# Output product of two channel mixers: gated values stationary, weights moving, 14 of 22 inner tiles in seven block products

## The chip, the cores and the metric

The kernel runs on one core of one Trainium2 chip. Its time is device time of one execution in microseconds (us). The engines are TensorE (PE: matmuls and their weight loads, PEld), VectorE (DVE), ScalarE (ACT), GpSimd (POOL) and SyncE (SP), which here issues most transfers. All matrix products are float32 work done as three products of parts: each operand is split into a high part (type fp32r) and the rest, and high x high, high x low and low x high are summed in PSUM.

## The reference

A trunk of two layers for 512 tokens of width 1024. Layer 0 mixes tokens by a recurrent scan beside a memory attention; layer 1 by chunked attention beside a memory attention. Each layer ends with the channel mixer, which is what the change is about:

```python
def conv_glu(h, w_in, conv_w, conv_b, w_out):
    gate, val = jnp.split(h @ w_in, 2, axis=-1)
    gp = jnp.pad(gate, ((0, 0), (CONV_W - 1, 0), (0, 0)))
    conv = conv_b + sum(conv_w[j] * gp[:, j:j + seq] for j in range(CONV_W))
    return (jax.nn.gelu(conv, approximate=False) * val) @ w_out
...
        x = x + jnp.concatenate([mix, mo], axis=-1) @ w_out[layer]
        x = x + conv_glu(rms_norm(x, ln2[layer]), ffn_in[layer], ffn_conv[layer],
                         ffn_conv_b[layer], ffn_out[layer])
    return rms_norm(x, ln_f)
```

The inner width is 2816 = 22 tiles of 128, so the last product of the mixer is a [512 x 2816] by [2816 x 1024] product.

## The kernel before

Everything is kept with features on partitions: the residual `xT` is [128, 8, 512], eight tiles of 128 features by 512 tokens. `ffn(l, ...)` is a generator that serves both layers. Its first half takes 21 of the 22 inner tiles through class `Seven`: for each tile seven block products of 128x256 stand for the gate and value products (lines 412 and 414), and a frame of hand-placed steps (`keep` pins their order on each queue) prepares the next tile's weights, while the gate chains of the tiles before (`end1` to `end5`: rho, three convolution taps, Gelu, times value) run on VectorE and ScalarE. The gated tiles are stored in float32: tiles 0 to 6 in `sp`, 7 to 13 in `x32[1]`, 14 to 21 in `x32[0]`. `rho`, the reciprocal root mean square of each token, is left out of the value branch and applied to the result.

`ending()` carries the last frame, the 22nd tile by plain products (`pg`, `pv`), the splits of all 22 gated tiles into high and low parts (`highs` on ScalarE, line 601; `lows` on VectorE, line 605), and the first weight units of the output product. Then the output product runs over the eight output tiles `m`: three units of weights with 7, 8 and 7 inner tiles are loaded (`raw_w`, line 192), split (line 173 on ScalarE, line 181 on VectorE, two units with an accumulating transfer at line 179), and `dense` multiplies them: weights stationary, gated values moving, 512 tokens wide, 66 matmuls for one `m` (lines 219, 220, 223). The result is multiplied by `rho` (line 731), added to `xT` (732), and `after(m)` squares and sums it for the next norm and, in layer 0, splits it for the queries of layer 1 (lines 270 to 278).

In layer 0 the attention layer begins behind that: two query projections of 24 matmuls each (`pq`), the norm's sums over features by matmuls with a column of ones (line 289), its transposes (302), the shared key and value operand (`kv_operand`), the key projection. In layer 1 `finish` takes the eighth tile in two halves of 256 tokens: the first half's norm and output run beside the second half's products (`store`), and the second half is turned by transposes (1731) and stored with tokens on partitions. So the two halves of the output have different layouts, which the host puts together.

[...] Split weights live in three buffers each of `whi` and `wlo`, 1024 columns long, raw weights in two of `wraw`. Outside the pinned stretches the framework orders each queue by priority (the order of the listing) among what its model holds ready.

Of the kernel before, what the change touches and what calls it, by code (L numbers as in the profile page):

```python
# [18 lines left out]
P = 128  # L19
S = 512  # L20
# [95 lines left out]
def trunk_kernel(ctx, tc, A, out):  # L116
# [278 lines left out]
    def ffn(l, hp, U, T, new_x, xT, after, last=None):  # L395
# [177 lines left out]
        hid = {}  # L573

        outs = {}
        UNITS = ((8, 7), (0, 8), (15, 7))

        def out_unit(m, u, pin=None):
            o, n = UNITS[u]
            src = A["ffn_out"][l, m][:, o * P:(o + n) * P]  # L580
            raw = raw_w(src, n * P)
            if m:
                return split_w(raw, n * P, None, pin or (lambda i: i)), list(range(o, o + n))
            return split_w(raw, n * P, src if u < 2 else None, keep, hold=True), list(range(o, o + n))

        def ending():
# [6 lines left out]
            hl = [hp.tile([P, 7, S], F32R, name="hl", tag="raw", bufs=2) for _ in range(2)]  # L593

            def place(k):
                return [t[:, k - 8] for t in hl] if k > 7 else (Th[:, k], Tl[:, k])

            def highs(*ks):
                for k in ks:
                    hid[k] = place(k) if k < 15 else (xh[:, k - 15], sl[:, k - 15])  # L600
                    keep(SC.copy(hid[k][0], hid32[k]))

            def lows(*ks):
                for k in ks:
                    keep(V.tensor_tensor(hid[k][1], hid32[k], hid[k][0], op=ALU.subtract))

            highs(8, 9)
# [3 lines left out]
            lows(8, 9)  # L611
# [4 lines left out]
            highs(10, 11, 12)  # L616
            lows(10)
            yield
            highs(13)
            yield  # L620
            pg = ps_f()
# [5 lines left out]
            lows(11)  # L627
            highs(0)
# [3 lines left out]
            highs(1, 14)  # L632
# [3 lines left out]
            lows(12)  # L636
            pv = ps_f()
# [7 lines left out]
            highs(7)  # L645
            u0 = out_unit(0, 0)
            u0[0][2]()
            lows(13, 14, 7)
            tile21.end3()
            tile21.end3b()  # L650
            highs(2, 3)
            lows(0, 1, 2)
            u1 = out_unit(0, 1)
            tile21.end4()
            highs(4, 5, 6)
            u1[0][2]()
            lows(3, 4, 5, 6)
            xh = new_x(1, F32R)
            sl = hp.tile([P, 7, S], F32R, name="sl", tag="sp")
            highs(15, 16, 17)  # L660
            tile21.end5()
            lows(15, 16, 17)
            u2 = out_unit(0, 2)
            highs(*range(18, NFF))
            lows(*range(18, NFF))
            u2[0][2]()
            outs[0] = [(w[:2], ks) for w, ks in (u0, u1, u2)]
            outs[1] = [out_unit(1, u, keep if u == 0 else None) for u in range(3)]
            yield

# [52 lines left out]
        for m in range(KD):  # L723
            us = outs[m] if m < len(outs) else [out_unit(m, u) for u in range(3)]
            if m == KD - 1 and last is not None:
                last(us, lambda k: hid[k])
                break
            ps = ps_d()
            run(dense(ps[:], us, lambda k: hid[k]))
            o = tmp()  # L730
            V.tensor_tensor(o[:], ps[:], rho[:], op=ALU.mult)
            V.tensor_tensor(xT[:, m], xT[:, m], o[:], op=ALU.add)
            after(m)
# [711 lines left out]
    def new_t():  # L1445
        return [hp.tile([P, KD, S], F32R, name="t" + u, tag="t" + u) for u in "hl"]

    mixer = ffn(0, hp, (r2h, r2l), new_t(), lambda i, dt: new_r(i, 1, dt), xT,
                lambda m: norm_tile(xT[:, m], m, "ln1_1", r2h, r2l))
    with fctx:  # L1450
        next(mixer)
# [391 lines left out]
```

## Time and profile before

| | |
|---|---|
| median of 3 runs | 1319.76 us (1319.14 to 1319.88) |
| profiled execution, its own time | 1320.44 us |
| its span | 1318.7 us |
| granted TensorE clock | 0.998 |
| PE busy | 1295.3 us (98%) |
| DVE busy | 980.1 us (74%) |
| ACT busy | 789.0 us (60%) |
| moved by DMA | 170.51 MB, mean 129 GB/s |

The span runs from the first to the last instruction of the profiled execution; its own time has some 1.7 us around that. A row of a timeline gives the start, the time, engine, line, operation, output and inputs, and in brackets the idle time before it with what ended it. A row of groups gives the count, the busy time and the mean of one in ns, then the idle time before. A duration of a matmul reaches to its modelled end; matmuls overlap, so the pace is read from starts.

### The profile page before, as it was taken

Reading aid. Unit: us, or ns where it says so; the run is one execution under the profiler, and the core shown is the slowest. Engines: PE = TensorE matmul, PEld = TensorE weight load, DVE = VectorE, ACT = ScalarE, POOL = GpSimd, SP = SyncE. Lnnn points to the kernel's source line nnn. Section 1 sums busy time; section 2 is a strip of 40 time slices with the busy share of each in tenths; the row PEclk is TensorE's granted clock in tenths of the full one; section 3 lists DMA queues with packets and bytes.
Section 4 is the critical chain, followed back from the end, with each engine's and each line's share of the span. In section 5 each row is a group of like instructions: output and inputs, shape, how many; then the busy total and the mean of one; then the engine's idle time right before and its main releaser. Section 6 shows DMA issues by size and latency. Waiting matters only on the chain.

```text
span 1318.7 us, 26462 instructions
## 1 busy us (share of the span) xinstructions
PE 1295.3 (98%) x10578; PEld 1122.7 (85%) x10578; DVE 980.1 (74%) x1933; ACT 789.0 (60%) x1318; POOL 113.2 (9%) x133
## 2 busy tenths in 40 slices
PE   9999999999999999999999999999999999999998
PEld 7887777767789999998888888787799999997887
DVE  7966867665689999999444666748889999995334
ACT  6656656655566776768223467757657767674321
POOL 0000000000001221220000000000012212200000
PEclk9999999999999999999999999999999999999999
DMA  6375344351236788776333432232447887855332
GB/s 200 109 191 112 88 90 104 87 114 58 95 97 160 178 198 183 173 174 150 106 99 107 136 98 79 86 107 88 128 105 178 197 180 175 198 126 139 101 99 78
DMA packets 87659, 170.51 MB, mean 129 GB/s; under 512 B 21232, under 2 KB 29552, under 8 KB 87536
## 3 DMA queue, kind: packets, MB, share of 16 engines
q1 hardware_dynamic: 67296, 124.94, 30.6%
q0 software_dynamic: 20240, 43.88, 19.8%
q8 instruction: 83, 1.36, 0.4%
q14 instruction: 40, 0.33, 0.1%
HBM read 152.57 MB, written 6.29 MB: 120 GB/s over the span
## 4 chain that ended last, share of the span: by engine, by line
PE 81%; ACT 7%; DVE 7%; DMA 2%; issue 2%; SPq 0%; DVEq 0%; ACTq 0%
PE psf L412 21%; PE psd L223 11%; PE psd L219 11%; PE psd L220 10%; PE psf L414 10%; PE pss L1593 1%; DVE wlo L181 1%; PE pss L1252 1%; PE psf L220 1%; PE psf L219 1%; PE pss L929 1%; ACT whi L173 1%; PE pss L1263 1%; PE pss L348 1%; PE psf L223 1%
## 5 line engine op out<-in xcount | busy, mean ns | idle before, releaser
L173 ACT CAST whi<-wraw 128x1024 fp32r<-128x1024 f32 (+1 forms) x116 | 118.0, 1020 | 198.5 <-DMA wraw<-in_ffn_out_dram 135.4
L181 DVE TENSOR_TENSOR wlo<-wraw,whi 128x1024 fp32r<-128x1024 f32 (+1 forms) x93 | 109.6, 1179 | 127.3 <-PE psd L223 72.4
L466 ACT CAST whi<-raw 128x1024 fp32r<-128x1024 f32 (+1 forms) x168 | 153.6, 941 | 71.7 <-PE psf L412 37.0
L412 PE MATMUL psf<-tl,whi 128*128 128x256 f32 x672 | 168.7, 283 | 0.0
L412 PE MATMUL psf<-th,whi 128*128 128x256 f32 x672 | 168.4, 283 | 0.0
L471 DVE TENSOR_TENSOR wlo<-raw,whi 128x1024 fp32r<-128x1024 f32 (+1 forms) x126 | 131.5, 1044 | 14.6 <-ACT whi L466 14.1
L412 PEld LDWEIGHTS psf<-tl,whi 128*128 128x128 f32 x672 | 128.9, 192 | 0.0
L412 PEld LDWEIGHTS psf<-th,whi 128*128 128x128 f32 x672 | 128.7, 192 | 0.0
L219 PE MATMUL psd<-r1h,whi 128*128 128x512 f32 x248 | 101.5, 410 | 0.1
L220 PE MATMUL psd<-r1l,whi 128*128 128x512 f32 x248 | 97.9, 396 | 0.0
L414 PE MATMUL psf<-th,wlo 128*128 128x256 f32 x504 | 81.2, 283 | 0.0
L223 PE MATMUL psd<-r1h,wlo 128*128 128x512 f32 x248 | 72.3, 407 | 0.0
L414 PEld LDWEIGHTS psf<-th,wlo 128*128 128x128 f32 x504 | 69.7, 192 | 0.0
L449 POOL DMA_DIRECT2D wlv<-in_ffn_in_dram x40 | 61.3, 1533 | 59.1 <-DVE tmp L533 58.3
L412 PE MATMUL psf<-r2h,whi 128*128 128x256 f32 x252 | 63.3, 283 | 0.5 <-ACT whi L466 0.5
L412 PE MATMUL psf<-r1h,whi 128*128 128x256 f32 x252 | 63.3, 283 | 0.5 <-ACT whi L466 0.5
L412 PE MATMUL psf<-r2l,whi 128*128 128x256 f32 x252 | 63.2, 283 | 0.0
L412 PE MATMUL psf<-r1l,whi 128*128 128x256 f32 x252 | 63.2, 283 | 0.0
L219 PEld LDWEIGHTS psd<-r1h,whi 128*128 128x128 f32 x248 | 46.5, 188 | 12.0 <-issue 2.8
L492 ACT ACTIVATE tmp<-tmp,vec 128x512 f32<-128x512 f32 x44 | 35.9, 816 | 34.1 <-DVE tmp L479 32.8
L220 PEld LDWEIGHTS psd<-r1l,whi 128*128 128x128 f32 x248 | 46.6, 188 | 8.1 <-issue 0.2
L223 PEld LDWEIGHTS psd<-r1h,wlo 128*128 128x128 f32 x248 | 44.1, 188 | 9.7 <-issue 1.2
(525 smaller groups left out, 3477.1 us busy)
## 6 DMA issues: line engine op xcount, KB each, us to landing
raw<-in_ffn_in_dram SPq DMA_DIRECT2D x42, 512.0 KB, 3.8
raw<-in_ffn_in_dram SPq DMA_DIRECT2D x84, 256.0 KB, 4.2
wlv<-in_ffn_in_dram POOLq DMA_DIRECT2D x40, 512.0 KB, 7.9
wraw<-in_ffn_out_dram SPq DMA_DIRECT2D x32, 448.0 KB, 3.4
wraw<-in_wA_dram SPq DMA_DIRECT2D x20, 512.0 KB, 4.0
wraw<-in_w_out_dram SPq DMA_DIRECT2D x16, 512.0 KB, 4.1
wraw<-in_ffn_out_dram SPq DMA_DIRECT2D x16, 512.0 KB, 3.5
wlo<-in_wA_dram POOLq DMA_DIRECT2D x15, 512.0 KB, 6.8
```

Of the source, the lines that this page charges most:

```text
L173: high = lambda: pin(SC.copy(hi[:, :n], raw))
L181: pin(V.tensor_tensor(lo[:, :n], raw, hi[:, :n], op=ALU.subtract))
L219: PE.matmul(ps, wh[:, j * P:(j + 1) * P], ah, start=start and n == 0, stop=False)
L220: dense_at[0] = PE.matmul(ps, wh[:, j * P:(j + 1) * P], al, start=False, stop=False)
L223: dense_at[0] = PE.matmul(ps, wl[:, j * P:(j + 1) * P], act(k)[0], start=False, stop=stop and n == len(ks) - 1)
L348: PE.matmul(pso[hs, :], vm[l][:, kt, (f * 2 + hh) * 64:(f * 2 + hh + 1) * 64], pts[f, hh, kt], start=kt == 0, stop=kt == 1)
L412: PE.matmul(ps, wh[:, o + k * P:o + k * P + P], x[k][n], start=k == n == 0, stop=False)
L414: PE.matmul(ps, wl[:, ol + k * P:ol + k * P + P], x[k][0], start=False, stop=k == 3)
L449: GP.dma_start(self.low[:].rearrange("p (a s) -> p a s", a=2), self.second, accum_op=ALU.add)
L466: keep(SC.copy(hi[:, :n], self.pair(what) if n > S else self.raw[:, what]))
L471: keep(V.tensor_tensor(lo[:, :n], self.pair(what) if n > S else self.raw[:, what], hi[:, :n], op=ALU.subtract))
L492: keep(SC.activation(self.c[:], self.g[:], AF.Identity, scale=Vc(f"cw2_{l}", self.j), bias=Vc(f"cb_{l}", self.j)))
```

## The change

In both layers the output product is computed by `out_by_seven`. The gated values become the stationary operand, 128 inner features by 128 tokens, and the weights move, 512 output features wide; a result block has 128 tokens on partitions and one half of the output features along the free axis. There are four token tiles (`th`, `t`) and two halves (`mh`).

- Inner tiles 0 to 6 and 21 are multiplied plainly (`plain`): for each half four chunks of two inner tiles, for all four token tiles.
- Inner tiles 7 to 20 form a 2 x 2 block problem: two inner halves of seven tiles, two token halves of 256, two feature halves of 512. It is done with seven block products (`seventh`: pm, pc, pa, pu, pd, pb, pe) in place of eight. Sums of gated blocks are made on VectorE, sums of weight blocks by accumulating transfers into `raw` and `rs` (`fetch`). Each product has four weight chunks (2, 2, 2 and 1 inner tiles), split into parts like before (`chunk`), and a gated operand split by `two_parts`.
- The factor `rho` is now one number for each partition (`nr`), applied as results are closed (`closed`, `scaled`).
- In `ending` only tiles 0 to 6 are split; `pg` and `pv` lie in `psd`.
- Layer 0: `Back.turn` transposes finished blocks and adds them to `xT`; `Back.post` splits and squares. The attention layer begins with inner tiles 0 to 3 of both query projections.
- Layer 1: `Tokens.rest` transposes `xT` and adds it to the blocks, `Tokens.out` norms each token over the free axis (Square with a running sum), multiplies by the gain, which is loaded in rows, and stores. The output has one layout. `finish` and `after` go.
- The host lays `ffn_out` out as `ffn_out7` (blocks) and `ffn_outp` (plain chunks).

```diff
@@ ending
-            hl = [hp.tile([P, 7, S], F32R, name="hl", tag="raw", bufs=2) for _ in range(2)]
...
-            pg = ps_f()
+            two_parts((Th, Tl), sp, keep)
+            pg = ps_d()
...
+        def fetch(raw, *names, add=False):
+            for name in names:
+                src = A["ffn_out7"][l, BLOCK[name]].rearrange("p (k s) -> p k s", k=7)
+                for k in range(0, 7, 2):
+                    ks = slice(k, min(k + 2, 7))
+                    if add:
+                        GP.dma_start(raw[:, ks], src[:, ks], accum_op=ALU.add)
+                    else:
+                        nc.sync.dma_start(raw[:, ks], src[:, ks])
+                add = True
...
+        def two_parts(hl, src, pin=lambda i: i):
+            n = src.shape[1]
+            for ks in (slice(0, 4), slice(4, n)):
+                pin(SC.copy(hl[0][:, ks], src[:, ks]))
+                pin(V.tensor_tensor(hl[1][:, ks], src[:, ks], hl[0][:, ks], op=ALU.subtract))
+
+        def chunk(raw, c, spare=False):
...
+                hi = wp.tile([P, 1024], F32R, name="whi", tag="whi")[:, :n * S]
+                lo = wp.tile([P, 1024], F32R, name="wlo", tag="wlo")[:, :n * S]
+            SC.copy(hi, s_)
+            V.tensor_tensor(lo, s_, hi, op=ALU.subtract)
+            return hi, lo, n
+
+        def rows(pss, act, k0, ch, first, last):
+            hi, lo, n = ch
+            for t, ps in pss:
+                ts = slice(t * P, t * P + P)
+                for i in range(n):
+                    for a in act:
+                        PE.matmul(ps[:], a[:, k0 + i, ts], hi[:, i * S:i * S + S],
+                                  start=bool(first) and (first is True or t in first) and a is act[0] and i == 0, stop=False)
+            for t, ps in pss:
+                ts = slice(t * P, t * P + P)
+                for i in range(n):
+                    PE.matmul(ps[:], act[0][:, k0 + i, ts], lo[:, i * S:i * S + S], start=False, stop=bool(last) and t in last and i == n - 1)
+
+        def seventh(pss, raw, act, first=True, last=True, read=None, side=()):
+            pss, side = list(enumerate(pss)), iter(side)
+            if read is None:
+                for c in range(4):
+                    rows(pss, act, 2 * c, chunk(raw, c), first and c == 0, (0, 1) if last and c == 3 else ())
+                    next(side, id)(0)
+                return
+            chs = [chunk(raw, c, True) for c in range(4)]
+            for p in pss:
+                for c in range(4):
+                    rows([p], act, 2 * c, chs[c], first and c == 0, (0, 1) if c == 3 else ())
+                    next(side, id)(0)
+                read(p[0])
...
+        def out_by_seven():
...
+            plain(pa + pb, 0, range(1), (0, 1, 2, 3))
+            fetch(raw, "g1")
+            plain(pa + pb, 0, range(1, 3), ())
+            fetch(rs, "v1", "v2")
+            two_parts(operand(Uh), hd(x0, h1))
+            pm = [ps_d() for _ in two]
+            seventh(pm, raw, operand(Uh))
+            fetch(raw, "g2")
+            V.tensor_tensor(hd(x0, h1), hd(x0, h2), hd(x0, h1), op=ALU.subtract)
+            two_parts(operand(Ul), hd(x0, h1))
...
+            pc = [ps_s() for _ in two]
+            seventh(pc, rs, operand(Ul))
+            fetch(rs, "g1", add=True)
+            two_parts(operand(Uh), hd(x1, h1))
+            split_to(Th[:, 7], Tl[:, 7], x1[:, 7])
...
+            plain(pa + pb, 0, (3,), (), ())
+            seventh(pa, raw, operand(Uh), first=False)
+            fetch(raw, "g1", "v1")
+            for t in two:
+                closed(0, t, 0, pa[t])
+            V.tensor_tensor(hd(x0, h1), hd(x0, h1), hd(x1, h2), op=ALU.subtract)
+            two_parts(operand(Ul), hd(x0, h1))
+            pu = [ps_d() for _ in two]
+            seventh(pu, rs, operand(Ul))
+            fetch(rs, "g2", add=True)
+            V.tensor_tensor(hd(x1, h1), hd(x1, h1), hd(x0, h1), op=ALU.add)
+            V.tensor_tensor(hd(x0, h2), hd(x0, h2), hd(x1, h2), op=ALU.subtract)
+            two_parts(operand(Uh), hd(x0, h2))
...
+            pd = [ps_f() for _ in two]
+            seventh(pd, raw, operand(Uh), side=side(0, 0))
+            two_parts(operand(Ul), hd(x1, h2))
...
+            seventh(pb, rs, operand(Ul), first=False)
+            fetch(rs, "v2")
+            for t in two:
+                closed(1, t, 0, pb[t])
+            sl = new_x(1, F32R)
+            two_parts(operand(sl), hd(x1, h1))
...
+            plain(pe + pc, 1, range(4), (0, 1, 2, 3), (2, 3), (2, 3, 0, 1), side(1, 1) if tokens else [id, *side(1, 0), lambda _: after.post((0, 1, 2, 3), slice(0, S))])
+            for t in two:
+                closed(1, t, 1, pc[t])
+            if tokens:
+                tokens.out(1, two, blk)
...
+            seventh(pe, rs, operand(sl), first=False, read=read,
+                    side=() if tokens else [id, id, *side(1, 1), lambda _: after.post((4, 5, 6, 7), h2)])
+            if not tokens:
+                after.post((4, 5, 6, 7), h1)
...
-        for m in range(KD):
-            us = outs[m] if m < len(outs) else [out_unit(m, u) for u in range(3)]
...
+        out_by_seven()
@@ class Back (layer 0)
+            for t in ts:
+                for i in range(4):
+                    PE.transpose(pss[i // 2][:, i % 2, t], blk(th, t, mh)[:, i * P:i * P + P], C("ident"))
+            if 1 in ts:
+                for n in range(2):
+                    x_ = xT[:, mh * 4 + n * 2:mh * 4 + n * 2 + 2, th * 256:th * 256 + 256]
+                    V.tensor_tensor(x_, x_, pss[n][:].rearrange("p m t c -> p m (t c)"), op=ALU.add)
...
@@ attention layer
-        run(dense(pq[0][:], [(first[0], K8)], act2))
+        for n in range(2):
+            run(dense(pq[n][:], [(first[n], K8)], act2, order=K8[0:4], stop=False))
+        run(dense(pq[0][:], [(first[0], K8)], act2, order=K8[4:8], start=False))
...
-        run(dense(pq[1][:], [(first[1], K8)], act2))
+        run(dense(pq[1][:], [(first[1], K8)], act2, order=K8[4:8], start=False))
@@ class Tokens (layer 1)
+            def rest(self, t, mh, o, op):
+                ps = ps_s()
+                for i in range(4):
+                    PE.transpose(ps[:, i * P:i * P + P], xT[:, mh * 4 + i, t * P:t * P + P], C("ident"))
...
+                    V.tensor_tensor(o, o, ps[:], op=op)
...
```

More of the change, by code (lines that the diff above doesn't have):

```diff
@@ L393, in trunk_kernel, with ffn @@
     T2, T3, T1, T4 = range(4)
-    def ffn(l, hp, U, T, new_x, xT, after, last=None):
+    def ffn(l, hp, U, T, new_x, xT, after=None, tokens=None):
         (Uh, Ul), (Th, Tl) = U, T
@@ new lines, in operand @@
+        def operand(t):
+            return t[:, 0:7, h1], t[:, 0:7, h2]
+        def two_parts(hl, src, pin=lambda i: i):
[4 more added lines that the diff above has]
+        def chunk(raw, c, spare=False):
+            n = 2 if c < 3 else 1
+            s_ = raw[:, 2 * c:2 * c + n].rearrange("p k s -> p (k s)")
+            if spare and c == 3:
+                t = wp.tile([P, 1024], F32R, name="wlv", tag="wraw", bufs=2)
+                hi, lo = t[:, 0:S], t[:, S:2 * S]
+            else:
+                hi = wp.tile([P, 1024], F32R, name="whi", tag="whi")[:, :n * S]
[3 more added lines that the diff above has]
+            return hi, lo, n
@@ L1755, in trunk_kernel @@
+        mixer = ffn(1, hp, (r1h, r1l), new_t(), lambda i, dt: new_r(i, 2, dt), xT, tokens=Tokens())
         next(mixer)
```

247 lines of the change are left out of this document (105 added, 142 removed).

## The prediction

> **What bounds the kernel now.** I read the page first (busy shares, then the chain that ended last), then the table of windows by stage.
>
> ```profile
> span 1318.7 us, 26462 instructions
> PE 1295.3 (98%) x10578; PEld 1122.7 (85%) x10578; DVE 980.1 (74%) x1933; ACT 789.0 (60%) x1318; POOL 113.2 (9%) x133
> ...
> PE 81%; ACT 7%; DVE 7%; DMA 2%; issue 2%; SPq 0%; DVEq 0%; ACTq 0%
> ```
>
> TensorE is busy 98% of the span and carries 81% of the chain: it is the bound wherever nothing else interrupts it. The stages that the change touches, one window each (columns: the window, its length, then each engine's busy time with its count):
>
> ```profile
> 380.00:600.00 220.00, 219.48 (x1786) 217.22 (x1785) 206.82 (x311) 149.38 (x196) 41.98 (x39) 1.00 0.71 165
> 600.00:616.00 16.00, 16.00 (x92) 14.06 (x91) 13.89 (x23) 12.41 (x20) 0.91 (x1) 1.00 0.45 128
> 616.00:632.10 16.10, 15.08 (x67) 11.98 (x66) 12.24 (x19) 11.27 (x19) 1.72 (x2) 1.00 0.71 163
> 632.10:736.80 104.70, 104.70 (x463) 86.70 (x462) 43.09 (x49) 33.45 (x43) 0.00 (x0) 1.00 0.34 97
> 736.80:749.50 12.70, 12.46 (x61) 10.10 (x60) 9.97 (x22) 4.92 (x6) 0.43 (x3) 1.00 0.77 260
> 1186.40:1202.50 16.10, 15.38 (x68) 12.24 (x67) 12.25 (x19) 11.28 (x19) 1.72 (x2) 1.00 0.71 162
> 1202.50:1292.20 89.70, 89.70 (x397) 74.33 (x396) 32.77 (x36) 25.59 (x31) 0.00 (x0) 1.00 0.34 97
> 1292.20:1310.00 17.80, 17.74 (x146) 17.33 (x146) 10.69 (x24) 3.90 (x7) 0.00 (x0) 1.00 0.20 76
> 1310.00:1318.70 8.70, 2.49 (x21) 2.02 (x19) 3.26 (x12) 1.65 (x3) 0.00 (x0) 0.88 0.33 123
> ```
>
> Row four is the output product of layer 0 from its second tile on: seven output tiles of 66 matmuls, 462 in 104.70 us, no idle time at all, so one matmul of 512 columns costs **0.2266 us**. Rows six to eight are layer 1 (six tiles in 89.70 us: the same). VectorE is busy there 43.09 of 104.70 us, so there is room. Row one, the first half of layer 0's mixer, shows VectorE at 206.82 of 220 us while PE still idles only 0.5 us: 94% on VectorE can be lived with where the order suits.
>
> ```profile
> 623.68 0.50 PE L219 MATMUL psd<-r1l,whi 128*128 128x512 f32 x1 [1.02 <-ACT whi L173]
> 1194.10 0.50 PE L219 MATMUL psd<-r2l,whi 128*128 128x512 f32 x1 [0.71 <-ACT whi L173]
> ```
>
> These are the only bubbles of the two output stages: the third weight unit waits in ScalarE's queue behind the splits of gated tiles.
>
> **Matmuls removed.** Before: 8 output tiles x 22 inner tiles x 3 = 528 per layer. After: the plain part is 2 halves x 8 inner tiles x 4 token tiles x 3 = 192; seven products of 7 inner tiles x 2 token tiles x 3 = 42 each are 294; together 486, all still 512 columns wide with one weight load each. So 42 fewer, 42 x 0.2266 = **-9.5 us per layer**; one product lasts 9.5 us.
>
> **Transposes added.** Results now have tokens on partitions and the residual does not. Layer 0 turns results back, layer 1 turns the residual over: 32 transposes each, in 8 groups of four.
>
> ```profile
> 749.17 0.60 PE L302 MATMUL pss<-cst,tmp 128*128 128x128 f32 x4
> 749.53 0.48 PE L219 MATMUL pss<-r1h,whi 128*128 128x512 f32 x1
> 749.84 0.40 PE L220 MATMUL pss<-r1l,whi 128*128 128x512 f32 x1
> ...
> L302 PE MATMUL pss<-cst,tmp x20: 270/272/327, 27.6 to 1304.8; 128*128 128x128 f32 x20
> ```
>
> Four transposes hold the stream 0.36 us, and the matmul behind them advances by 0.31 instead of 0.23, so a group costs 0.44: 8 x 0.44 = **+3.5 us per layer** (0.36 if the switch were free).
>
> **Layer 1's ending.** Its eighth tile in two halves, woven with the norm, takes 17.80 us instead of 104.70/7 = 14.96: that form goes, **-2.8**. The tail:
>
> ```profile
> 1309.08 1.00 PE L223 MATMUL psd<-r2l,wlo 128*128 128x256 f32 x7
> 1310.12 0.38 ACT L1726 ACTIVATE tmp<-psd 128x256 f32<-128x256 f32 x1 [4.62 <-PE psd L223]
> 1311.39 0.17 DVE L245 TENSOR_SCALAR rsqy<-fa 128x2 int32<-128x2 int32 x1
> 1312.65 0.16 DVE L1746 TENSOR_TENSOR ff<-rsq,early 128x2 f32<-128x2 f32 x1
> 1315.01 0.39 SPq L1752 DMA_DIRECT2D out_dram<-wraw  x1
> ```
>
> The last dense matmul starts near 1309.9, so 8.8 us follow it. After: matmul latency 0.4, closing operation 0.75, Square with sum 0.65, the small chain 1.6 (1.42 from L245 to L1746, and one more), two gain multiplications 1.5, then 3.7 from the last issue to the end, as here: 8.6. I take **0**, within 0.5 either way.
>
> **Bubbles.** The splits of all 22 gated tiles that crowd the window 600-632 fall to those of seven, so I drop both: **-1.0 and -0.7**.
>
> **The way into the attention layer.** Windows row five: from the last output matmul to the key projection 12.70 us, VectorE busy 9.97, so 2.7 idle.
>
> ```profile
> L731 DVE TENSOR_TENSOR tmp<-psd,rho 128x512 f32<-128x512 f32 x7 | 4.8, 691 | 1.8 <-PE psd L223 1.8
> L732 DVE TENSOR_TENSOR xT<-xT,tmp 128x512 f32<-128x512 f32 x7 | 4.8, 692 | 0.2
> L278 DVE SCALAR_TENSOR_TENSOR r2l<-xT,vec,r2h 128x512 fp32r<-128x512 f32 x7 | 5.2, 748 | 0.3 <-ACT r2h L277 0.3
> L181 DVE TENSOR_TENSOR wlo<-wraw,whi 128x1024 fp32r<-128x1024 f32 x9 | 11.0, 1226 | 14.6 <-PE psd L223 12.1 <-ACT whi L173 2.4
> L173 ACT CAST whi<-wraw 128x1024 fp32r<-128x1024 f32 x9 | 9.5, 1051 | 21.2 <-DMA wraw<-in_ffn_out_dram 16.0 <-DMA wraw<-in_wB_dram 2.8 <-PE psd L220 2.5
> 1300.83 0.42 DVE L1701 TENSOR_TENSOR xT<-xT,tmp 128x256 f32<-128x256 f32 x1
> 1310.54 0.48 DVE L1727 SCALAR_TENSOR_TENSOR tmp<-psd,vec,rho 128x256 f32<-128x256 f32 x1 [2.44 <-ACT tmp L1726]
> ```
>
> Before, four operations on the last tile follow the last matmul (0.69+0.69+0.75+0.69 = 2.8 us). After, there are a closing one (0.75), two adds of turned results (1.4) and, for four tiles of half the tokens, a split (0.48) and a sum (0.42) each (3.6): 5.7. TensorE meanwhile has inner tiles 0-3 of both query projections, 24 x 0.2266 = 5.4 us, and the first split is due after some 3.8, so the projections themselves are covered. The 2.9 us more on VectorE against 2.7 idle leave between 0 and 2.9 for the key projection: I take **+1.0**, nearer to the covered end.
>
> **VectorE inside the stage.** This is the real question. By the rows: a chunk of 1024 is 1.23, one of 512 is 0.69, so by slope 7 x 256 elements are 2.0 (an estimate). A product's four chunks take 4.4, splitting its gated operand 2.2, a sum of blocks 2.0, a result operation 0.7. Take the third to fifth product (pa, pu, pd): PE 3 x 9.5 + 4 x 0.44 = 30.3 us. VectorE must do in that time ten full and half chunks of these and two of the next (13.1), two operands (4.4), the two closings (1.5), six adds (4.1), two to four turned adds (1.4 to 2.8): 24.5 to 25.9. Three sums and pu's operand (8.2) have their inputs earlier, when the plain chunk gives VectorE some 4 us and the products pm and pc leave more; if none is pulled forward, 32.7 to 34.1, which is 3.8 too much. The weight buffers hold three chunks, 2.7 us of PE each, so a delay under 3 us is absorbed. Bounds 0 and 3.8 per layer; I take 1.0. The last product holds all its chunks; the third gets its buffer only when the plain part ends, and the closings of the other half (1.5), in layer 1 also the norm chain and four multiplications (4.6), come ahead of it: bounds 0 and 2.5, I take 1.0. Together **+2.0 per layer**.
>
> Whether work is pulled forward, the queue shows:
>
> ```profile
> 737.01 0.69 DVE L731 TENSOR_TENSOR tmp<-psd,rho 128x512 f32<-128x512 f32 x1 [0.31 <-PE psd L223]
> 737.62 0.74 DVE L278 SCALAR_TENSOR_TENSOR r1l<-xT,vec,r1h 128x512 fp32r<-128x512 f32 x1
> 738.27 0.68 DVE L732 TENSOR_TENSOR xT<-xT,tmp 128x512 f32<-128x512 f32 x1
> ```
>
> The key operand's split, listed after the query projection, sits between two operations that are listed before it: the order is one of readiness, not of the listing.
>
> **Transfers.** Block sums come from accumulating transfers.
>
> ```profile
> q0 software_dynamic: 20240, 43.88, 19.8%
> ...
> raw<-in_ffn_in_dram SPq DMA_DIRECT2D x42, 512.0 KB, 3.8
> wlv<-in_ffn_in_dram POOLq DMA_DIRECT2D x40, 512.0 KB, 7.9
> ```
>
> Per layer the SP queue now issues 8 plain chunks and 20 block pieces, POOL 16 accumulating pieces: 4.2 + 9 x 1.8 = 20.7 MB over some 114 us, 180 GB/s where the window 632-737 moved 97. Row one lives with 165 beside a full PE, and on SP nothing else waits but the plain chunks, which have two buffers ahead. The tightest is g1+v1 for pd: a piece is free once pa's chunk is split, then 3.8 + 7.9 = 11.7 us, and pd needs it two products (19 us) later. The queue's 43.88 MB took 19.8% of 1318.7 us, 3.1 us a piece, so four pieces overlap. Cost **0**; bad end in the third rival.
>
> **Sum.** Layer 0: -9.5 + 3.5 - 1.0 + 1.0 + 2.0 = -4.0. Layer 1: -9.5 - 2.8 + 3.5 - 0.7 + 2.0 = -7.5. Rounded terms kept, **-11.6 us**. The profiled execution took 1320.44, 0.7 above the median of 1319.76; it would take 1308.8, and the median becomes **1308.2**.
>
> **Rivals.** *No stalls:* everything ready in time, -11.6 - 4.0 - 1.0 = -16.6, **1303.2**; with transposes at 0.36 a group 1301.9. For it: row one at 94% without a bubble.
> *VectorE falls behind:* 3.8 + 2.5 us per layer and 2.9 on the way out, -16.6 + 12.6 + 2.9 = -1.1, **1318.7**; halfway, 1311 to 1316. For it: 32.7 against 30.3.
> *Listing order (slower):* VectorE and ScalarE keep each product's results ahead of the next one's weights. Then at a boundary PE waits for closings 1.5, a sum 2.0, an operand 2.2 and a chunk 1.2, some 7 us. Five boundaries a layer give 70 us, less the 11.6 and with the 4.0 replaced: **1374**. It decides from about three boundaries on; the three rows of L731, L278, L732 speak against it.
> *Late block sums (slower):* if accumulating pieces go one by one at 7.9 us, g1+v1 ends 3.8 + 31.6 = 35 us after its start; its last piece is due after 19 + 6 = 25, so it is 10 late, and the next sum in the same queue 20 more: 60 us, **1368**. It decides when a piece holds the queue over 5.3 us ((25 - 3.8)/4); the trace's share gives 3.1. [...]
> *Transposes do not pipeline:* at the 272 ns of one, 64 cost 17.4 us instead of 7.0: -1.2, **1318.6**. [...]
>
> **Numbers.** Forecast 0.55, no stalls 0.14, VectorE behind 0.14 (half of it faster, 0.04 same, 0.03 slower), listing order 0.10, late sums 0.04, transposes 0.03. A measurement can tell about 0.2%, 2.6 us. Faster 0.55+0.14+0.07 = 0.76; same 0.07; slower 0.17. The range, 1302 to 1322, runs from no stalls with the cheaper transposes to VectorE behind with the first boundary of the listing order; beyond lies some 0.17.
>
> **What would show it.** 486 matmuls of 512 columns per output stage at 0.227 us; eight groups of transposes at 0.44; VectorE near 80-85% there; idle PE of a few us waiting for whi or wlo. PE waiting for raw or rs means the transfers; waits of 7 us at each product, the listing order; over 16 us of bubbles in all would make the forecast wrong in sign.

## The result: 3 us faster, not 12

The changed kernel takes **1316.53 us** (median of 9 runs, 1315.35 to 1318.23), the kernel before 1319.76 on the same chip (9 runs): ratio 0.9978, 95% interval 0.9967 to 0.9988. The profiled execution took 1316.99 with a span of 1315.2, against 1320.44 and 1318.7. The forecast was 1308.2: the sign was right and the time lies in the range, but of the 11.6 us some 3 came. That it lies in the range is in part luck: the 4.0 us allowed for stalls inside the stages, which did not come, make up for a part of the costs that were not foreseen.

The head of the profile after:

```profile
span 1315.2 us, 26403 instructions
PE 1283.5 (98%) x10460; PEld 1103.8 (84%) x10460; DVE 1039.5 (79%) x1978; ACT 822.0 (63%) x1354; POOL 137.6 (10%) x161
```

118 matmuls fewer in all, 11.8 us less busy time on TensorE, but only 3.5 us less span: the difference is waiting. The table of windows shows where. First the kernel before, from wg's first matmul to the first output matmul of each layer (the "entrance"), then the kernel after: first half, entrance, output stage and the way to the key projection in layer 0, then entrance, stage and tail of layer 1. The columns are those of the prediction's first table.

```profile
604.80:615.70 10.90, 10.90 (x50) 9.01 (x49) 9.91 (x17) 7.31 (x12) 0.00 (x0) 1.00 0.46 154
1175.50:1186.40 10.90, 10.90 (x50) 9.03 (x49) 9.75 (x16) 7.16 (x11) 0.00 (x0) 1.00 0.43 144
```

```profile
380.00:600.00 220.00, 219.48 (x1786) 217.03 (x1785) 206.00 (x311) 148.76 (x195) 41.98 (x39) 1.00 0.74 172
604.90:618.50 13.60, 11.43 (x50) 8.80 (x49) 7.39 (x8) 4.39 (x5) 1.46 (x3) 1.00 1.03 283
618.50:732.70 114.20, 114.17 (x515) 93.91 (x516) 86.88 (x96) 63.23 (x83) 11.12 (x13) 1.00 0.57 137
732.70:745.70 13.00, 13.00 (x66) 10.44 (x64) 11.34 (x29) 10.69 (x19) 0.43 (x3) 1.00 0.65 213
1176.60:1190.80 14.20, 11.61 (x51) 8.72 (x49) 7.16 (x7) 4.10 (x5) 1.54 (x3) 1.00 1.04 284
1190.80:1306.70 115.90, 115.90 (x518) 94.24 (x518) 85.08 (x101) 59.55 (x80) 11.15 (x13) 1.00 0.57 141
1306.70:1315.20 8.50, 0.24 (x2) 0.00 (x0) 5.14 (x18) 0.72 (x2) 0.00 (x0) 0.63 0.33 124
```

- **Stage, layer 0:** 114.2 us where it was 121.1 (615.70 to 736.81): -7.0, TensorE never idle, VectorE busy 86.88 of 114.2.
- **Entrances:** 13.6 and 14.2 us for the same 50 matmuls that took 10.9: +2.7 and +3.3. The DMA engines are at 1.03 and 1.04 of their time, where they were at 0.46 and 0.43.
- **Exit, layer 0:** from the first query matmul behind the output stage to the first frame of layer 1's mixer 229.7 us (732.67 to 962.37) against 224.4 (736.81 to 961.22): +5.3.
- **Stage and tail, layer 1:** 124.4 us against 132.3: -7.9. But the stage takes 1.7 longer than layer 0's.

The waits of TensorE in these stretches (in brackets the idle time and what ended it):

```profile
609.55 2.11 PE L223 MATMUL psd<-r2h,wlo 128*128 128x512 f32 x8 [0.79 <-DMA wlo<-in_ffn_in_dram]
...
618.53 0.50 PE L657 MATMUL psf<-whi,th 128*128 128x512 f32 x1 [1.41 <-ACT whi L173]
...
750.95 2.14 PE L223 MATMUL pss<-r1h,wlo 128*128 128x512 f32 x8 [0.82 <-DVE wlo L181]
...
755.68 0.38 PE L1671 MATMUL pss<-wlo,r1h 128*128 128x256 f32 x1 [2.59 <-DVE wlo L181]
...
1181.82 2.13 PE L223 MATMUL psd<-r1h,wlo 128*128 128x512 f32 x8 [1.35 <-DMA wlo<-in_ffn_in_dram]
...
1190.79 0.50 PE L657 MATMUL psf<-whi,th 128*128 128x512 f32 x1 [1.24 <-ACT whi L173]
```

None is inside an output stage. Each stands where the new stage meets its neighbour: at the entrance a weight that the DMA engines deliver late, at the exit a low part that VectorE makes late.

VectorE's load inside the stage cost nothing, and the order in which it worked fits that. The prediction counted three sums and the splitting of pu's gated operand, 8.2 us, that might not be pulled forward. In layer 0 all of it ran before the third product, pa, begins at 659.72 (the last row is the second half of the operand's split):

```profile
633.26 2.02 DVE L734 TENSOR_TENSOR r1l<-r1l,r1h 128x1792 f32<-128x1792 f32 x1
638.45 2.02 DVE L728 TENSOR_TENSOR r1l<-r1l,r1h 128x1792 f32<-128x1792 f32 x1
649.96 2.03 DVE L733 TENSOR_TENSOR r1h<-r1h,r1l 128x1792 f32<-128x1792 f32 x1
656.81 0.96 DVE L636 TENSOR_TENSOR r2l<-r1l,r2l 128x768 fp32r<-128x768 f32 x1 [0.28 <-ACT r2l L635]
```

### The profile page after: what moved, and what is told of

Same layout as the page of the kernel before. It is cut to its first block, busy times and chain, and to the rows that moved or that the text cites. A ratio compares the mean times of both kernels' runs of the same rounds, so it can differ in the third digit from the quotient of the medians.

```text
span 1315.2 us, 26403 instructions
## 1 busy us (share of the span) xinstructions
PE 1283.5 (98%) x10460; PEld 1103.8 (84%) x10460; DVE 1039.5 (79%) x1978; ACT 822.0 (63%) x1354; POOL 137.6 (10%) x161
## 5 line engine op out<-in xcount | busy, mean ns | idle before, releaser
L466 ACT CAST whi<-raw 128x1024 fp32r<-128x1024 f32 (+1 forms) x168 | 152.5, 941 | 67.8 <-PE psf L412 37.3
L471 DVE TENSOR_TENSOR wlo<-raw,whi 128x1024 fp32r<-128x1024 f32 (+1 forms) x126 | 131.5, 1044 | 14.3 <-ACT whi L466 14.2
L173 ACT CAST whi<-wraw 128x1024 fp32r<-128x1024 f32 x84 | 87.6, 1047 | 79.7 <-PE psd L220 27.5
L219 PE MATMUL psd<-r1h,whi 128*128 128x512 f32 x264 | 108.6, 412 | 0.0
L220 PE MATMUL psd<-r1l,whi 128*128 128x512 f32 x264 | 104.8, 398 | 0.0
L647 ACT CAST whi<-raw 128x1024 fp32r<-128x1024 f32 (+1 forms) x54 | 51.7, 957 | 64.5 <-PE psf L657 45.2
L181 DVE TENSOR_TENSOR wlo<-wraw,whi 128x1024 fp32r<-128x1024 f32 x65 | 79.3, 1220 | 14.9 <-ACT whi L173 14.4
L648 DVE TENSOR_TENSOR wlo<-raw,whi 128x1024 fp32r<-128x1024 f32 (+1 forms) x54 | 59.0, 1104 | 36.3 <-ACT whi L647 19.3
L223 PE MATMUL psd<-r1h,wlo 128*128 128x512 f32 x264 | 77.2, 409 | 1.4 <-DMA wlo<-in_ffn_in_dram 1.4
L219 PEld LDWEIGHTS psd<-r1h,whi 128*128 128x128 f32 x264 | 49.5, 188 | 13.1 <-issue 2.6
```

Source lines behind the costliest of these rows:

```text
L173: high = lambda: pin(SC.copy(hi[:, :n], raw))
L181: pin(V.tensor_tensor(lo[:, :n], raw, hi[:, :n], op=ALU.subtract))
L219: PE.matmul(ps, wh[:, j * P:(j + 1) * P], ah, start=start and n == 0, stop=False)
L220: dense_at[0] = PE.matmul(ps, wh[:, j * P:(j + 1) * P], al, start=False, stop=False)
L223: dense_at[0] = PE.matmul(ps, wl[:, j * P:(j + 1) * P], act(k)[0], start=False, stop=stop and n == len(ks) - 1)
L466: keep(SC.copy(hi[:, :n], self.pair(what) if n > S else self.raw[:, what]))
```

## The experiments

Ratios are against the kernel before, run on the same chip in the same rounds. There are three groups, each on another chip. The first four runs below are one (median of the kernel before 1318.07). The one tile moved back, the two edits with all tiles together, that kernel with the low part by VectorE and the first of the two with weight tiles apart are the second (1318.85). The rest are the third (1318.55). Between groups the ratios are compared, not the times.

### Entrance and exit

Three theories stood after the traces: transfers that start too early crowd the entrance; the exit's order on VectorE is wrong; or neither, and the stage itself has too much for VectorE. The changed kernel was run again beside them.

> The changed kernel once more, for a second trace of it beside the edits below. Its first trace has seven-product stages of 114.1 us in layer 0 and 115.9 us in layer 1, though both issue the same matmuls: in layer 1 a block product of 42 matmuls takes 9.79 us, in layer 0 9.52. Theory 'one execution': the slower pace belongs to that execution, and here layer 1 shows 9.52 too. Theory 'place': it belongs to layer 1 (other tiles, other transfers beside it), and 9.79 comes again. Time by both: 1316.5, within 1.5 us.

**1315.68 us**, ratio 0.9981 (0.9972 to 0.9990): the base for the next three. Its trace has stages of 114.2 and 115.8 us again, so the slower pace of layer 1 does not belong to one execution.

**Block fetches behind.** The first three block transfers are issued behind the raw transfer of the second plain chunk (`raw_at[0]` holds the last transfer that `raw_w` issued):

```
-            fetch(raw, "g1")
-            plain(pa + pb, 0, range(1, 3), ())
-            fetch(rs, "v1", "v2")
+            plain(pa + pb, 0, range(1, 2), ())
+            behind = raw_at[0]
+            plain(pa + pb, 0, range(2, 3), ())
+            with tc.issue_after(behind.ins):
+                fetch(raw, "g1")
+                fetch(rs, "v1", "v2")
```

> One edit: the first block transfers (g1, then v1 and the accumulated v2) are queued behind the raw weights of the second plain chunk, instead of as soon as their buffers are free. Theory 'entrance': in the changed kernel they crowd the last frame's own transfers (DMA share 1.0 from 600 to 617 us), so the 22nd tile and the first plain chunk wait: 0.8 and 1.4 us in layer 0, 1.35 and 1.24 in layer 1, and the stage starts 2.8 and 3.3 us later than before. Then these waits go, the product pm still finds g1 in time, and the time falls by 5 to 6.5 us, to about 1310.5. Rival 'pinned splits': the waits come from the two big splits of tiles 0 to 6 that stand ahead in the queues of ScalarE and VectorE; then moving the transfers changes under 1 us.

**1308.21 us**, 0.9925 (0.9912 to 0.9937): 7.5 us less than the changed kernel. The DMA issues between 598 and 622 us (KB each, median us from issue to landing), first in the kernel after, then here, with a window over the entrance below them:

```profile
raw<-in_ffn_out_dram SPq DMA_DIRECT2D x3, 512.0 KB, 5.2
raw<-in_ffn_out_dram POOLq DMA_DIRECT2D x3, 512.0 KB, 10.0
wraw<-in_ffn_outp_dram SPq DMA_DIRECT2D x3, 512.0 KB, 8.1
wlo<-in_ffn_in_dram POOLq DMA_DIRECT2D x1, 512.0 KB, 7.2
```

```profile
wraw<-in_ffn_outp_dram SPq DMA_DIRECT2D x3, 512.0 KB, 4.6
wlo<-in_ffn_in_dram POOLq DMA_DIRECT2D x1, 512.0 KB, 5.6
...
605.00:617.20 12.20, 12.20 (x61) 10.31 (x61) 11.35 (x13) 6.58 (x8) 0.00 (x0) 1.00 0.64 205
```

A plain chunk lands in 4.6 us and not 8.1, and TensorE has no idle time in layer 0's entrance, which takes 10.9 us as before the change; layer 1's takes 11.8. Nobody needed the blocks so early: with the fetches later, their products still never wait. The rival (the two big splits that stand ahead in the queues) allowed under 1 us, so it falls.

**Key weights first.** In the attention layer the key projection's weights are loaded and split ahead of the query products, the first value weights ahead of the split of the queries:

```
         first = [load_w(A["wB"][i]) for i in range(2)]
+        kw = load_w(A["w_kvk"][0])
...
         run(norm)
+        vw = [load_w(A["w_kvv"][0, u]) for u in range(2)]
         for i in range(2):
             q_split(pq[i], Tb[i])
-        run(chain(k_proj(0, Tb[0]), v_proj(0)))
+        run(chain(k_proj(0, Tb[0], kw), v_proj(0, vw)))
```

> One edit, in the way out of layer 0: the key projection's weights are listed before the query products and the first value weights before the query splits, so that their splits stand ahead of the key operand's on ScalarE and VectorE. Theory 'order at the exit': in the changed kernel TensorE waits 0.8 us for the key weights' low part and 2.6 us for the value weights', and then runs some 1.7 us' worth at a lower granted clock (0.95 over the next 34 us); all three go and the time falls by 4 to 5 us, to about 1312. Rival 'VectorE has too much to do there': the waits move to other operands behind them, and under 1.5 us is gained.

**1311.77 us**, 0.9952 (0.9940 to 0.9965): 3.9 less. The waits at 750.95 and 755.68 are gone; one of 0.58 us is left. The exit takes 225.5 us and not 229.7. In the kernel after, the order on VectorE (start, duration) had been this:

```profile
744.51 4.06 DVE L278 SCALAR_TENSOR_TENSOR r1l<-xT,vec,r1h 128x512 fp32r<-128x512 f32 x6
748.49 1.28 DVE L1630 SCALAR_TENSOR_TENSOR tmp<-psd,rho 128x512 f32<-128x512 f32 x2
749.68 1.22 DVE L181 TENSOR_TENSOR wlo<-wraw,whi 128x1024 fp32r<-128x1024 f32 x1
750.93 2.84 DVE L1635 TENSOR_TENSOR qs<-tmp,qs 64x512 fp32r<-64x512 f32 x4
753.80 0.69 DVE L1644 TENSOR_TENSOR tmp<-pss,rho 128x512 f32<-128x512 f32 x1
754.41 1.22 DVE L181 TENSOR_TENSOR wlo<-wraw,whi 128x1024 fp32r<-128x1024 f32 x1
```

The low parts that TensorE waits for (L181) stand behind the key operand's splits and the query splits. Before the change, output tiles came one after another, and most of that work was done inside the stage.

> Both edits. If entrance and exit are separate places the gains add: 1316.5 - 6 - 4.5 = about 1306, which is near the forecast's own sum without waits inside the stage. If both theories are wrong it stays above 1314.

**1306.16 us**, 0.9899 (0.9884 to 0.9915): 9.5 less, where the single gains sum to 11.4. In its profile wg's accumulated low part in layer 1 comes late, a wait of 1.93 us.

### The pace of layer 1's products

A product takes 9.52 us in layer 0 (0.2266 us a matmul) and 9.80 in layer 1 (0.2333), in every profile up to here and at a granted clock of 1.00. Its operands there are r1h and r1l. And layer 0's last product, whose operand lies in r1l, was slow too (median 396 ns a matmul in the kernel after), while layer 1's last, in r2l, was fast (389): the pace goes with the tile, not with the layer. In the compiled program before, r1h, r1l and the tiles of all later pools start 32 bytes past a multiple of 128. The change replaces three small tiles by two in the pool behind r1h and r1l, so every later pool, with the weight tiles in it, moved by 32 bytes and they did not. One edit moves it back:

```
-                self.ss = cp.tile([P, 8], F32, name="ss")
+                self.ss = cp.tile([P, 16], F32, name="ss")
```

> The changed kernel with one edit: the tile ss of 32 bytes is made 64 bytes. It lies in the pool in front of everything but r1h and r1l, so all tiles behind it move by 32 bytes. In the kernel before, r1h, r1l and all the later tiles start 32 bytes past a multiple of 64; the change's own small tiles moved the later ones to a multiple of 64, and left r1h and r1l where they were; this edit puts all of them back. Theory (offset): a matmul of 512 columns whose stationary and moving operands start at different places within 64 bytes takes 0.2333 us and not 0.2266, one of 256 columns 0.1180 and not 0.1200. Expected: layer 1's products 9.80 -> 9.52 us (six, -1.7), layer 0's last product 9.8 -> 9.52 (-0.3), the 512-column matmuls on r1h and r1l between 720 and 960 us -1.2 (some 190), layer 1's first half +1.6 (750 matmuls of 256 columns), the 790 matmuls on r1h before 400 us 0 to -5, taken at 0 because both kernels reach 600 us together. Sum about -1.5 against the changed kernel, 1314.5 beside 1315.7 to 1316.5. Rival (what lies beside it in layer 1, its transfers or its side work, slows the products): they keep 9.80 and the time doesn't change.

**1314.11 us**, 0.9960 (0.9946 to 0.9973), 2.8 less than the changed kernel run again by the ratios, though the two intervals touch. Of the parts expected, the 1.2 us between 720 and 960 us did not show: the exit takes 229.7 us in both profiles. The pace leaves no doubt. By tile, minimum/median/maximum ns of one matmul, in layer 1's first product and then on r1h elsewhere, with 512 and with 256 columns; the kernel after, then this one:

```profile
L657 PE MATMUL psd<-whi,r1h x28: 392/395/397, 1207.5 to 1216.6; 128*128 128x512 f32 x28
...
L219 PE MATMUL psd<-r1h,whi x264: 388/396/505, 19.0 to 1187.1; 128*128 128x512 f32 x132
...
L412 PE MATMUL psf<-r1h,whi x252: 277/280/385, 962.4 to 1175.9; 128*128 128x256 f32 x126
```

```profile
L657 PE MATMUL psd<-whi,r1h x28: 389/389/389, 1207.4 to 1216.2; 128*128 128x512 f32 x28
...
L219 PE MATMUL psd<-r1h,whi x264: 387/389/505, 18.6 to 1185.0; 128*128 128x512 f32 x132
...
L412 PE MATMUL psf<-r1h,whi x252: 277/283/386, 959.4 to 1174.2; 128*128 128x256 f32 x126
```

In these rows operands 32 bytes apart cost 6 to 7 ns with 512 columns, whichever of the two is stationary, and save 3 with 256.

The same done to the kernel before, by 32 bytes ahead of r1h and 32 behind r1l:

> The kernel before, with r1h and r1l moved by 32 bytes against all tiles behind them, as the change did by accident. Theory (offset): 512-column matmuls on r1h and r1l get 0.2333 us for 0.2266: before 390 us +2.5 (790 matmuls, about half on the path by the other kernels), the hidden parts that lie in r1l in layer 0's mixer +1.1 (168), between 720 and 960 us +0.7 to 1.2, layer 1's wg and wv +0.3; its first half gets 0.1180 for 0.1200, -1.7. Sum +3, so about 1321.5 beside 1318.5. Rival (the place matters only for the new form of matmul, tokens stationary): no change.

**1321.63 us**, 1.0022 (1.0013 to 1.0031), slower by the 3 us expected. The profiled execution, 1319.65, is the fastest of its eleven, so that the profile shows the pace and not the sum. The same form of matmul:

```profile
L414 PE MATMUL psf<-r1h,whi x252: 277/281/386, 960.8 to 1173.0; 128*128 128x256 f32 x126
...
L221 PE MATMUL psd<-r1h,whi x248: 387/396/503, 18.7 to 897.0; 128*128 128x512 f32 x124
```

So the rival (only the new form of matmul) falls. Then the same two small tiles in the kernel with both edits, so that all tiles lie together:

> The kernel with both edits (block fetches behind, key weights first), and r1h and r1l moved by 32 bytes so that they too start at a multiple of 64, as all others in it do. Theory (offset): the same -1.5 against that kernel, about 1304.5; layer 1's products at 9.52 us, layer 1's first half at 0.1200 us a matmul again. Rival (what lies beside): products keep 9.8, about 1306.

**1302.39 us**, 0.9876 (0.9858 to 0.9894): 3.0 less by the ratios than with both edits alone, twice what was expected, with intervals that overlap a little; the products are at 9.52 us. Not all of it is the place of the tiles: the wait of 1.93 us that stood in the other profile is absent in this one, so that layer 1's entrance takes 10.9 us and not 14.9.

> As the kernel with all at a multiple of 64, and the low part of the last tile's first weights is made by VectorE and not by an accumulating transfer. Theory (the two edits together missed the sum of their gains by 1.9 us because that transfer came 1.93 us late in layer 1): the wait goes, -1.5 to -1.9, about 1303. Rival (the rest is elsewhere, VectorE's added 1.1 us makes another wait): 1304.5 to 1306.

Here `wg = split_w(raw_w(src[0]), 1024, None, keep, hold=True)` takes the place of the accumulating form. **1301.75 us**, 0.9869 (0.9855 to 0.9883): not told apart from the kernel above, which in its own profile no longer had the wait that this was to remove. This is the fastest kernel of the study. The missing 1.9 us of the two edits are thus explained by one trace only, not shown by an edit. The gains may also overlap: the trace with the fetches behind had an exit 0.7 us shorter than the kernel after, with the key weights still late (229.0 against 229.7).

**Apart on purpose.** If operands apart are good for 256 columns, the first halves could gain. Weight tiles get 16 floats more; the frames use them from float 8 on, all else from 0 (`[:, 8:1032]` and `[:, :1024]`):

> As the kernel before it in this call (all at a multiple of 64), but the weights of the first half of both channel mixers start 32 bytes past one, so that its 256-column matmuls have operands at different places. Theory (offset, the sign depends on the width): the 3500 matmuls there take 0.1180 and not 0.1200 us, -7, so about 1297.5. Rivals: only a moving operand that lies apart shortens them, then no change, 1304.5; or the place of the weights lengthens them by 3 per cent as in the products, +12, 1317.

**1306.21 us**, 0.9901 (0.9887 to 0.9915): slower than the kernel with all together, a miss for every case listed. The first halves' matmuls did get shorter (from 393 to 595 us TensorE was busy 200.44 us with 1686 matmuls, where the kernel with all together had 201.48 with 1679), but the products went to 9.70 to 9.77 us though their offsets within 64 bytes agree: buffers of 4160 bytes begin at 64 and at 0 within 128 by turns, and the gated operands at 64.

> All at one offset, key weights first, block fetches behind and the low part by VectorE, and again the first half's weights 32 bytes apart, but with weight buffers of 4224 bytes and not 4160. In the kernel with 4160 the buffers began at 64 and at 0 within 128 bytes by turns, and the products ran at 0.2266 us from the one and at 0.2325 from the other. Theory (what counts is the offset within 128 bytes or more): the products go back to 9.52 us; the first half's matmuls keep 0.1180, but VectorE, busy 95 per cent there, lets only 1 to 2.5 us of their 7 through: 1299.5 to 1301 beside 1301.8. Rival (the weights' moved places slow the products in themselves): products stay at 9.72 to 9.77, about 1305.

**1304.08 us**, 0.9886 (0.9872 to 0.9899): a miss again. Products at 9.64 to 9.67. In its stream, eight matmuls of a chunk take 1.83, 1.82 and 1.87 us by the starts of what follows:

```profile
628.61 1.99 PE L661 MATMUL psd<-whi,r2h 128*128 128x512 f32 x8
630.44 1.07 PE L666 MATMUL psd<-wlo,r2h 128*128 128x512 f32 x4
631.34 1.98 PE L661 MATMUL psd<-whi,r2h 128*128 128x512 f32 x8
633.16 1.09 PE L666 MATMUL psd<-wlo,r2h 128*128 128x512 f32 x4
634.08 2.03 PE L661 MATMUL psd<-whi,r2h 128*128 128x512 f32 x8
635.95 1.10 PE L666 MATMUL psd<-wlo,r2h 128*128 128x512 f32 x4
```

Buffers of 4224 bytes begin at 192, 64 and 192 within 256, r2h at 192, and two of these three chunks are fast. The author takes the chunk of 1.87 us for the one with 128 bytes between its operands; the trace gives its time, not its place, and how far the effect goes was not tried. The first halves gained 1.5 us a layer (223.5 against 225.0 in layer 0, from the first frame to the first output matmul), the products lost 0.12 to 0.15 each; in the profiles the rest of the loss stands ahead of layer 0's first frame (1.0 us) and at the exit (0.4). Other matmuls of 512 columns use the same buffers there, but that was not tried by itself.

### Layer 1 alone, and more work for VectorE

> The changed kernel with all tiles back at one offset (ss of 64 bytes), but layer 0's channel mixer, its norm and the query products behind it as in the kernel before: the change in layer 1 alone. Theory (by the traces the change loses in layer 0, where the faster stage pays for a later entrance and a later exit): from the first frame of layer 0 to that of layer 1 the kernel with the change in both layers took 571.6 us, the kernel before 570.5, so leaving layer 0 as it was gains 1.2 us against it: about 1313, beside 1314.1. Rival (the forecast's own division, 4.0 us of gain in layer 0): 1318.

Layer 0's mixer, its norm and the query products are the old code. **1313.02 us**, 0.9955 (0.9943 to 0.9968), against 1314.11 (0.9960) with the change in both layers: the 1313 of the theory, not the 1318 of the forecast's division. From the first frame of layer 0 to that of layer 1 it takes 570.5 us, as before the change. In layer 0, as written, the change earned nothing.

```
             SC.copy(hi, s_)
-            V.tensor_tensor(lo, s_, hi, op=ALU.subtract)
+            for _ in range(1 if c % 2 else 2):
+                V.tensor_tensor(lo, s_, hi, op=ALU.subtract)
```

> The kernel with both edits and all at one offset, and in the channel mixers' second half two of the four chunks of every block product make their low parts twice on VectorE: 14 instructions of 1.2 us more per layer, 17 us. Theory (TensorE holds the stage alone: VectorE was busy 82.6 of 113.4 us in it and TensorE all 113.4): the added work goes into VectorE's free time, 0 to +2 us in all, 1302.5 to 1304.5. Rival (the forecast's: work of VectorE in the stage comes late for the matmuls that wait for it, 2 us a layer at the load it has): with 17 us more it grows to 4 us or more a layer, 1307 or more.

**1305.26 us**, 0.9895 (0.9881 to 0.9908), some 2.5 more than without by the ratios, whose intervals overlap a little: between the two. Layer 0's stage takes 117.3 us in the profile and not 113.5, layer 1's 114.6 and not 113.8. The first 113.4 us of layer 0's stage, without and with the added work:

```profile
613.60:727.00 113.40, 113.40 (x515) 93.76 (x514) 82.59 (x91) 60.85 (x80) 13.87 (x16) 1.00 0.67 174
```

```profile
613.60:727.00 113.40, 111.51 (x497) 91.77 (x496) 95.33 (x100) 58.34 (x75) 13.88 (x16) 0.98 0.66 172
...
687.64 2.02 PE L667 MATMUL psf<-wlo,r2l 128*128 128x512 f32 x4 [1.89 <-DVE wlo L653]
...
688.00:690.00 2.00, 2.00 (x6) 1.54 (x6) 2.00 (x3) 0.95 (x2) 0.00 (x0) 0.50 0.65 168
690.00:692.00 2.00, 2.00 (x8) 1.58 (x7) 2.00 (x3) 0.00 (x0) 0.00 (x0) 0.71 0.27 102
```

Of the added work, 13 us in this window, TensorE felt one wait of 1.89 us, and in layer 1 one of 0.66, both in the product pb. So VectorE held up the stage here, where it was busy some 84% of the time (95.33 of 113.4); in the change it is at 76% (86.88 of 114.2).

## Why the forecast was wrong, step by step

- **Matmuls, transposes, ending, tail, bubbles of the stage: right.** Without stalls they say -9.5 + 3.5 - 1.0 = -7.0 for layer 0's stage; measured -7.0. For layer 1 -9.5 + 3.5 - 2.8 - 0.7 = -9.5; measured -7.9, and the pace of r1h and r1l takes six times 0.28 = 1.7 of it. One of layer 0's eight groups of transposes falls behind the stage (733.92), so the agreement is good to some 0.4. The transposes pipelined, as the sum had it: in the kernel after one lasts 272 ns (median of 28), but four hold the stream for 0.35 us in all (725.70 to 726.05).
- **"Transfers. Cost 0": the step that failed first, 6.0 us.** It set the transfers of the whole stage against its whole length, and asked when each block is needed. It did not ask when they start: as soon as a buffer is free, in front of the transfers that the entrance waits for (in layer 0 four block pieces are issued from 588.28 us on and more from 598.35, while the last frame runs to 604.95). "On SP nothing else waits but the plain chunks" was the wrong sentence: the plain chunk itself was late, and with it the split that the stage begins with. The bubbles dropped at 623.68 and 1194.10 came back as others. Moving the three fetches returned 7.5 us. Another reading there was loose without harm: 3.1 us of a piece against 7.9 to its landing let two or three pieces overlap, not four; the sums were in time all the same.
- **"The way into the attention layer, +1.0": mis-sized, +5.3 measured, outside its bounds of 0 to 2.9.** It summed VectorE's work against its idle time up to the key projection's first matmul, and that interval hardly moved (13.0 us against 12.7). What it left out lies behind it: the order, in which low parts that TensorE needs stood behind splits that it needs later (0.82 and 2.59 us), and a lower clock after the wait (0.57 over four us; 0.7 us by two traces, below). Key weights first brought the exit from 229.7 to 225.5 us; the 1.1 left against the kernel before hold one group of transposes (0.44) and the wait of 0.58.
- **"VectorE inside the stage, +2.0 per layer": 0 measured.** The rival without stalls was right on the stage; the work was pulled forward, as the three rows in the prediction suggested and the four rows above show. With 13 us more of it in layer 0's stage TensorE waited once, 1.89 us.
- **The pace of 0.2266 for every product: not a step, but an assumption.** Where tiles come to lie was no part of the forecast; it cost 1.7 us in layer 1's products and 0.3 in layer 0's last. What it cost or gave in old matmuls is not settled.

In sum, against -11.6: entrances +6.0, exit +4.3 (5.3 less the 1.0 allowed), pace +1.7, stalls -4.0, rounded rest +0.1: -3.5, the difference of the two profiled spans. With the three costs taken away the kernel came to 1302.39, 0.8 us from the 1303.2 of the rival without stalls (by the ratio to its own kernel before, 0.2 from it). The rivals of listing order, late block sums and a VectorE that is behind did not occur: inside the stages of the kernel after no matmul waited for a block or for VectorE.

## What to carry to other kernels

Price a new stage at its two seams as well as inside: list what it issues before it begins (here block transfers were issued from 588.28 us on, and the last frame ran to 604.95), and what the work that follows used to have done during the stage that is replaced. Look at the granted clock behind a wait in each profile: a wait of 1.89 us had 0.50 and 0.71 behind it and its stage grew by 3.8 us; of two waits of 2.59 us one had 0.57 behind it, the other 1.00. After any change of tiles, even of small ones, compare the pace of unchanged matmuls: the places of their operands may have moved against each other, as here by 32 bytes (0.2333 us for 0.2266).

## What the runs showed of the hardware

**The clock after a wait.** The wait of 2.59 us at 755.68 in the kernel after, by windows:

```profile
753.00:756.00 3.00, 0.41 (x3) 0.32 (x3) 2.94 (x5) 1.44 (x3) 0.00 (x0) 1.00 0.27 111
756.00:760.00 4.00, 4.00 (x23) 4.00 (x22) 3.50 (x5) 2.81 (x4) 0.00 (x0) 0.57 0.41 131
```

The granted clock is 0.57 over the four us behind it, by the author's estimate worth 1.7 us (0.43 x 4.0) of TensorE's work. Behind the wait of 1.89 us in the kernel with more VectorE work it was 0.50 and then 0.71, over two us each, and that stage grew by 3.8 us in all, twice the wait. Behind the wait of 1.93 us in the kernel with both edits it was 0.50 from 1174 to 1176 and 0.69 over the next two us. But the length of a wait doesn't settle it. In the kernel with the block fetches behind, a wait as long at the same place left the clock at 1.00:

```profile
753.92 0.39 PE L1676 MATMUL pss<-wlo,r1h 128*128 128x256 f32 x1 [2.59 <-DVE wlo L181]
...
753.00:756.00 3.00, 2.08 (x17) 2.07 (x17) 2.94 (x5) 2.92 (x5) 0.00 (x0) 1.00 0.35 59
756.00:760.00 4.00, 3.69 (x29) 3.36 (x28) 3.33 (x5) 2.82 (x4) 0.00 (x0) 1.00 0.47 150
```

Its exit took 229.0 us against 229.7: the two traces differ by 0.7 us, not by 1.7. At one place in layer 0 the kernel before has a clock of 0.59 behind 2.04 us without a matmul, the kernel after 1.00 behind 1.41:

```profile
296.59 0.26 PE L1132 MATMUL pss<-cst,KB 64*128 64x64 f32 x1 [2.04 <-issue]
...
297.00:300.00 3.00, 3.00 (x33) 2.83 (x31) 0.00 (x0) 1.48 (x4) 0.00 (x0) 0.59 0.11 22
```

```profile
296.41 0.21 PE L1231 MATMUL pss<-cst,KB 64*128 64x64 f32 x1 [1.41 <-issue]
...
297.00:300.00 3.00, 3.00 (x37) 2.33 (x35) 0.00 (x0) 2.25 (x7) 0.00 (x0) 1.00 0.10 28
```

Which waits lower the clock stays open.

**Operands apart.** In these runs a matmul's pace went with where its two operands start against each other. With 32 bytes between them it was 0.2333 us and not 0.2266 at 512 columns (layer 1's products at 9.80 and 9.52 us, before and after the edit that moved the tiles back), and 0.1180 and not 0.1200 at 256 (on r1h and r1l eight in 0.94 us from 972.14 on in the kernel after, in 0.96 from 970.99 on in the kernel before). With longer weight buffers eight matmuls of 512 columns took 1.86, 1.81 and 1.86 us in r2h's product and 1.86 to 1.87 in r2l's (4160 bytes), and 1.83, 1.82 and 1.87 in r2h's (4224 bytes); that the slower ones have 64 and 128 bytes between their operands is the author's reading of the buffers' places. Why the sign turns with the width stays open.
